# Half of a gMLP's u projection as seven Strassen block products, and one set of operand forms built two tiles earlier

## The chip, the cores and the metric

The kernel runs on one core of a Trainium2 chip. The metric is the device time of one launch in microseconds (us). Measurements of this kernel agree with each other to about 0.03%; 0.2% of its time, 3.9 us, is taken here as what can be told from no change.

The engines of the core: TensorE (PE in the profile, with PEld for its weight loads), VectorE (DVE), ScalarE (ACT), GpSimd (POOL) and SyncE (SP), which starts the transfers. Every engine works through its own list of instructions in order and waits on semaphores of the others.

## The reference

A decoder trunk with two layers over 544 columns: 512 of a prompt and 32 of a sample (8 sequences of 4). Only the part around the change matters here:

```python
h = h + 0.5 * swiglu(rmsnorm(h, ffn1_norm[i]), ffn1_w1[i], ffn1_w3[i], ffn1_w2[i])
xn = rmsnorm(h, mix_norm[i])                 # layer 0: the gMLP mixer
u, v = jnp.split(xn @ w_in, 2, axis=-1)      # w_in: 1024 x 2048
v = rmsnorm(v, v_norm)                       # v of the sample is an output too (gmlp_v_sample)
s = jnp.einsum('gts,bnsgd->bntgd', ws, vg)   # per chunk of 128 positions, lower triangle
h = h + (u * (s + b_s)) @ w_out
h = h + 0.5 * swiglu(rmsnorm(h, ffn2_norm[i]), ffn2_w1[i], ffn2_w3[i], ffn2_w2[i])
```

Layer 1 has attention in place of the mixer. All arithmetic is to be as exact as float32.

## The kernel before, in words

Everything is held transposed: a 1024-wide activation is 8 tiles of 128 features by 544 columns. A float32 product is made of three fp32r matmuls, high parts by high parts (line L285), high by low (L289) and low by high (L291), for each of 8 slices of 128 inputs and each of the two halves of 272 columns. A plain output tile of 128 features thus takes 48 matmuls of 272 columns, all added up in one PSUM buffer of the pool `ps`. This pool has three buffers of two banks; a second pool `pb` has two of one bank.

Weights come as tiles of 128 x 1024 by transfers that SP starts (L208), and are split ahead of their use: ACT rounds to the high part (L241), DVE subtracts to get the low part (L242). `self.ahead` holds how many such units ahead the split, the sums of blocks and the load stand.

The feed-forward parts (FFN) use Strassen's scheme (in Winograd's form) for their wide products: seven products of blocks, called "1", "5", "6", "2", "7", "3", "4" in the order of the work, give four output tiles of 128 x 544, each product being 24 matmuls (L538) instead of the 32 that they would share of eight. Three accumulators are used: A (a `ps` buffer; products 1, 6, 7, 4, one after the other into the same sums), C (a `ps` buffer; 5, then 3) and B (the two `pb` buffers; 2). After "1", "5" and "6" ACT copies the accumulator out (L546) before the next product may add to it. After "2", "7" and "3" DVE adds such a copy to the sums (L553, L555, L557), and after "4" ACT copies the result out (L560). The four block weights are plain pieces; the other three are sums of these, made on DVE (L227). The right-hand operand needs "forms", sums of the blocks of the activations: `forms()` makes them for two feature tiles at a time, by 2 ACT scalings (L351), 3 DVE sums (L355, L357, L358), 2 ACT casts and 2 DVE subtractions (L329, L330). There are four such sets per FFN. The first FFN of a layer-0 pass and its second are preceded by two plain pairs of tiles (`plain=2`: four plain tiles, copied by ACT at L471), and `more()` spreads the sets of forms over these tiles.

The gMLP (`gmlp`) works in this order:
- the eight v tiles, each taken out of PSUM by DVE with the norm's factor (L644), and squared by ACT for v's own norm (L368, summed by POOL at L370);
- the u tiles 0, 1, 2 (L656), then two transposes of v tiles (`v_turn`: each five small matmuls, L665 and L666, into a `ps` buffer, copied out by ACT at L668 and L669);
- the u tiles 3 to 7 with between them the other transposes and the spatial products (`spatial`: L676 and L679 on PE, L687, L690 and L694 on DVE);
- the eight output tiles (L714 adds them to the residual), which at once prepare the second FFN (`on_chunk`), its forms 1 to 3 among them.

DVE multiplies v by its norm's factor (L659), and takes the sample's 32 columns of each v tile (L661) into a small buffer of a pool of four, from where SP sends them out (`out_gv`).

Outside the FFN's product steps a list scheduler sets the order of each engine's instructions; within the product steps the order is as written.

Of the kernel before, what the change touches and what calls it, by code (L numbers as in the profile page):

```python
# [29 lines left out]
P = 128  # L30
# [62 lines left out]
def turns(out):  # L93

    return out.rearrange("p (b a) -> p b a", a=2)
# [42 lines left out]
class Builder:  # L138
# [207 lines left out]
    def forms(self, h, gcol, n, xs):  # L346

        nc = self.nc
        x = self.big()
        for a in range(2):  # L350
            nc.scalar.activation(x[:, a, :], h[2 * n + a], AF.Copy, scale=self.gain(gcol + 2 * n + a))  # L351
        t13, t24 = self.tmp(), self.tmp()
        two = lambda t: t.rearrange("p (a b) -> p a b", a=2)
        f13, f24 = self.big(F32R), self.big(F32R)
        nc.vector.tensor_tensor(two(t13), x[:, :, HT:], two(x[:, 0, :]), ALU.subtract)  # L355
        self.split_pair(f13, t13)
        nc.vector.tensor_tensor(t24[:, :HT], x[:, 1, HT:], t13[:, :HT], ALU.subtract)  # L357
        nc.vector.tensor_tensor(t24[:, HT:], x[:, 1, :HT], t24[:, :HT], ALU.subtract)  # L358
        self.split_pair(f24, t24)
        half = lambda t, b: tuple(x[:, b * HT:(b + 1) * HT] for x in t)  # L360
        f13, f24 = ((t[:, 0, :], t[:, 1, :]) for t in (f13, f24))
        return {"1": half(xs[2 * n], 0), "2": half(xs[2 * n + 1], 0), "3": half(xs[2 * n + 1], 1),
                "5": half(f13, 0), "7": half(f13, 1), "6": half(f24, 0), "4": half(f24, 1)}
    def ssq(self, acc, h, cols=slice(0, T), first=False):

        nc = self.nc
        sq = acc[:, cols] if first else self.tmp()[:, cols]
        nc.scalar.activation(sq, h[:, cols], AF.Square)  # L368
        if not first:
            nc.gpsimd.tensor_tensor(acc[:, cols], acc[:, cols], sq, ALU.add)  # L370
# [80 lines left out]
    def ffn(self, h, box, gcol, rstd, on_chunk, plain=1):  # L451

        nc, eng = self.nc, mybir.EngineType
        self.ahead = (2, 3, 6)
        first, xs, xf = [], self.pairs(box), box["f"]

        def more(n):
            if len(xf) < min(n, NKP):
                xf.append(self.forms(h, gcol, len(xf), xs))
        hid, todo = {}, ([], [])  # L460
        lead = plain == 1 and len(xf) < 3
        for f in range(2 * plain):
            g = self.big()
            for w in range(2):
                if lead:
                    more(len(xf) + 1)
                if rstd is None:
                    p, rstd = self.tile_rstd(xs, box["acc"])
                else:
                    p = self.tile_mm(xs)  # L470
                nc.scalar.copy(halves(g[:, w]), whole(p))  # L471
                for t in todo:
                    if t:
                        t.pop(0)()
                if not lead:
                    more((2 * f + w + 1) // plain)
            first.append((f // 2, f % 2, g))
            if f % 2 and f < 2 * plain - 1 or lead and f == 0:
                for j, a, g in first:
                    todo[a].extend(self.gate(hid, rstd, j, a, g))  # L480
                first = []
        assert self.chain is None
        for j, a, g in first:
            todo[a].extend(([None] * 3 if j == 0 else []) + self.gate(hid, rstd, j, a, g))
        with self.tc.manual_schedule(engines={eng.PE, eng.Activation, eng.DVE, eng.Pool}):
            self.ffn_steps(h, xf, rstd, hid, todo, plain, on_chunk)
        self.ahead = (2, 2, 4)
        self.pins = 2
        return rstd
# [127 lines left out]
    def gmlp(self, h, box, on_chunk):  # L617
# [13 lines left out]
        for g in range(NH):  # L631
            nc.gpsimd.tensor_tensor(wss[:NS, g * NS:(g + 1) * NS], wss[:NS, g * NS:(g + 1) * NS],
                                    self.c[:NS, C_TRI4:C_TRI4 + NS], ALU.mult)
        rstd, sq, v = None, self.st(), []
        for c in range(NC_):
            if rstd is None:
                p, rstd = self.tile_rstd(xs, box["acc"])
            else:
                p = self.tile_mm(xs)
            if c % 2 == 0:  # L640
                vt = self.big()

            def take(p=p, vc=vt[:, c % 2, :]):
                nc.vector.tensor_tensor(halves(vc), whole(p), halves(rstd), ALU.mult)  # L644
                self.ssq(sq, vc, first=not v)
                v.append(vc)
            self.evac(take)
        m, us = [None] * NC_, {}
        vts = {}

        def u_tile(c):
            p = self.tile_mm(xs)
            if c % 2 == 0:
                us["t"] = self.big()
            us[c] = us["t"][:, c % 2, :]
            nc.vector.tensor_tensor(halves(us[c]), whole(p), halves(rstd), ALU.mult)  # L656

        def v_turn(c):
            nc.vector.tensor_tensor(v[c], v[c], rv, ALU.mult)  # L659
            vs = self.sm(NS)  # L660
            nc.vector.tensor_scalar(vs, v[c][:, SEQ:], self.gain(G_GV + c), None, ALU.mult)  # L661
            nc.sync.dma_start(out=self.o["gv"][c], in_=vs)
            t = self.ps()
            for j in range(4):
                nc.tensor.transpose(t[:, 0, j * P:(j + 1) * P], v[c][:, j * P:(j + 1) * P], self.ident)  # L665
            nc.tensor.transpose(t[:NS, 1, :P], v[c][:, SEQ:], self.ident)  # L666
            vt = self.big()
            nc.scalar.copy(vt[:, 0, :SEQ], t[:, 0, :])  # L668
            nc.scalar.copy(vt[:NS, 1, :P], t[:NS, 1, :P])  # L669
            vts[c] = (vt[:, 0, :], vt[:, 1, :])  # L670
# [25 lines left out]
                self.split_pair(pair, sg)  # L696
                m[c] = pair[:, 0, :], pair[:, 1, :]

        u_tile(0)
        rv = self.rstd(sq)  # L700
        u_tile(1)
        u_tile(2)
        assert self.chain is None
        v_turn(0)
        v_turn(1)
        for c, spatials, turns in ((3, (0,), (2, 3)), (4, (1,), (4,)), (5, (2, 3), (5,)), (6, (4, 5), (6, 7)),
                                   (7, (6, 7), ())):
            u_tile(c)
            for k in turns:
                v_turn(k)  # L710
            spatial(*spatials)
        for c in range(NC_):
            p = self.tile_mm(m)
            nc.vector.tensor_tensor(halves(h[c]), whole(p), halves(h[c]), ALU.add)  # L714
# [655 lines left out]
    def build(self):  # L1370
# [3 lines left out]
        def plain(aps):  # L1374
            for ap in aps:
                self.add_plain(ap)

        def ple_units(n):
            for c in range(NC_):
                self.add_plain(i["wg"][n, c])  # L1380
                if c < 2:
                    self.add_plain(i["wp"][n, c])

        self.ffn_pieces(0)
        plain([i["win"][NC_ + c] for c in range(NC_)] + [i["win"][c] for c in range(NC_)])
        plain(i["wout"][c] for c in range(NC_))
        self.ffn_pieces(1)
        ple_units(0)
# [87 lines left out]
def _stationary(w):  # L1476

    k, m = w.shape
    return np.ascontiguousarray(
        w.reshape(k // P, P, m // P, P).transpose(2, 1, 0, 3).reshape(m // P, P, k // P * P))  # L1480
# [5 lines left out]
    return w.reshape(k // 256, 2, P, m // 256, 2, P).transpose(3, 4, 1, 2, 0, 5).reshape(m // 256, 4, P, k // 256, P)  # L1486


def _constants():
    c, d = np.zeros((P, NCONST), np.float32), np.zeros((P, NPASS), np.float32)  # L1490
    r = np.arange(P)
    c[:, C_ID:C_ID + P] = np.eye(P)
    d[:, C_NEG + P:C_NEG + 2 * P] = np.where(r[None, :] > r[:, None], NEG, 0.0)
    d[:, C_TRI:C_TRI + P] = r[:, None] <= r[None, :]
    d[:, C_TRI + P:C_STRICT] = 1
    d[:, C_STRICT:C_STRICT + P] = r[:, None] > r[None, :]
    d[:, C_PICK:C_PICK + NH] = r[:, None] % NS == NQ * np.arange(NH)[None, :]
    b4, hd, q = r // 32, r // 4 % 8, r % 4
    for k in range(4):
        c[:, C_ROLE + k] = q == k  # L1500
    c[:, C_ROLE + 4] = -(q == 0).astype(np.float32)
    c[:, C_ROLE + 5] = -(q == 1).astype(np.float32)
    c[:, C_ROLE + 6] = q >= 2
    c[:, C_ROLE + 7] = q < 2
    c[:, C_ROLE + 8] = hd == b4
    c[:, C_ROLE + 9] = hd == b4 + 4
    for k in range(4):
        c[:, C_B4 + k] = b4 == k
        c[:, C_SEL + k] = q == k
        c[:, C_NEGQ + k] = np.where(k > q, NEG, 0.0)  # L1510
    for k in range(8):
        c[:, C_H + k] = hd == k
    s = np.arange(NS)
    c[:, C_SUM:C_SUM + NS] = r[:, None] % NS == np.arange(NS)[None, :]
    c[:NS, C_TRI4:C_TRI4 + NS] = (s[:, None] // 4 == s[None, :] // 4) & (s[:, None] <= s[None, :])
    d[P - NS:, C_TRI4S:C_TRI4S + NS] = c[:NS, C_TRI4:C_TRI4 + NS]
    return c, d


def _arrays(x_prompt, x_sample, p_prompt, p_sample, cache_k, cache_v, cache_logf, page_table, ffn1_norm, ffn1_w1,  # L1520
# [9 lines left out]
    for w1, w3, w2, n in ((ffn1_w1, ffn1_w3, ffn1_w2, 0), (ffn2_w1, ffn2_w3, ffn2_w2, 0),  # L1530
# [9 lines left out]
    a["wp"] = np.stack([_stationary(w).reshape(2, 4, P, 2 * P).transpose(0, 2, 1, 3).reshape(2, P, 8 * P)  # L1540
                        for w in ple_w_proj])
    a["win"], a["wout"] = _stationary(gmlp_w_in[0]), _stationary(gmlp_w_out[0])
    a["wk"] = _stationary(w_kvf[:, :D])

    a["wv"] = w_kvf[:, D:2 * D].reshape(2, 4, P, 4, 256).transpose(3, 0, 2, 1, 4).reshape(8, P, 1024)
# [50 lines left out]
```

## Time and profile before

| | before |
|---|---|
| median of 3 runs | 1931.98 us (1931.47 to 1932.03) |
| the profiled execution | 1931.48 us, its span 1929.7 us |
| TensorE's granted clock over the span | 1.00 |
| PE busy, DVE busy, ACT busy in the span | 1906.5, 1457.5, 950.2 us |
| first FFN | to 356 us of the span |
| gMLP: v tiles; u tiles, transposes and spatial products; output tiles | 356 to 401; to 462; to 506 us |
| second FFN: plain tiles; product steps | from 506; from 529 us |

Times of instructions are counted from the span's start. A row of the timeline holds start, duration, engine, line, operation, output and input, and in brackets the idle time of this engine before it with what ended it. A row of the waits holds what waited for what, the sum, the count and the longest. A row of windows holds, for each of PE, PEld, DVE, ACT and POOL, the busy time and the number of instructions, then the granted clock, the share of the transfer engines and their rate.

### The profile page before, as it was taken

What the parts mean: (1) busy time and instruction counts of PE and PEld (TensorE: products, weight loads), DVE (VectorE), ACT (ScalarE), POOL (GpSimd) and SP (SyncE); (2) the same over time, 40 slices, a digit from 0 to 9 for tenths busy, and PEclk for the clock granted to TensorE, in tenths of its full rate; (3) what the DMA queues carried; (4) which work ended last, traced back from release to release, by engine and by line L of the source; (5) the groups of instructions that cost most, each with busy time, mean ns of one, the idle gap of its engine ahead of it and who ended that gap; (6) DMA issues with size and microseconds to landing.
All of it is one profiled execution on the core that took longest, in us unless ns stands there. A gap on an engine that the chain in (4) does not pass through costs nothing.

```text
span 1929.7 us, 39007 instructions
## 1 busy us (share of the span) xinstructions
PE 1906.5 (99%) x16508; PEld 1872.2 (97%) x16508; DVE 1457.5 (76%) x1799; ACT 950.2 (49%) x1396; POOL 142.6 (7%) x190
## 2 busy tenths in 40 slices
PE   9999999999999999999999999999999999999999
PEld 8999999999999999999999999999977899999999
DVE  7887877556788877766578887877476888878774
ACT  7544434424554444454466454444374754444461
POOL 0000000410100000023000000001131300000020
PEclk9999999999999999999999999999999999999999
DMA  5233234312223233431484232324769332332431
GB/s 195 79 112 121 84 123 147 108 48 88 88 88 107 86 120 105 153 104 45 144 306 157 103 129 69 129 86 136 217 210 341 101 110 81 112 113 86 139 109 47
DMA packets 98048, 237.62 MB, mean 123 GB/s; under 512 B 12130, under 2 KB 29826, under 8 KB 97874
## 3 DMA queue, kind: packets, MB, share of 16 engines
q1 hardware_dynamic: 97730, 235.09, 36.9%
q8 instruction: 130, 2.13, 0.5%
q14 instruction: 44, 0.36, 0.1%
q10 hardware_dynamic: 144, 0.04, 0.0%
HBM read 218.65 MB, written 16.44 MB: 122 GB/s over the span
## 4 chain that ended last, share of the span: by engine, by line
PE 89%; DVE 6%; ACT 3%; issue 1%; DMA 1%; POOL 0%; SPq 0%; ACTq 0%; DVEq 0%; POOLq 0%
PE ps L538 31%; PE ps L285 15%; PE ps L291 15%; PE ps L289 15%; PE pb L538 5%; DVE big L242 2%; ACT big L241 1%; DVE big L227 1%; DMA big<-in_cv 1%; PE ps L891 1%; PE ps L892 1%; PE ps L893 1%; DVE big L496 0%; DVE big L330 0%; PE ps L1285 0%
## 5 line engine op out<-in xcount | busy, mean ns | idle before, releaser
L538 PE MATMUL ps<-big,big 128*128 128x272 f32 x5616 | 668.8, 279 | 5.9 <-DVE big L555 3.5
L538 PEld LDWEIGHTS ps<-big,big 128*128 128x128 f32 x5616 | 658.5, 189 | 7.0 <-issue 4.0
L242 DVE TENSOR_TENSOR big<-big,big 128x1024 fp32r<-128x1024 f32 (+2 forms) x505 | 582.8, 1157 | 93.4 <-ACT big L241 92.9
L241 ACT CAST big<-big 128x1024 fp32r<-128x1024 f32 (+2 forms) x505 | 483.1, 977 | 326.5 <-DVE big L227 251.9
L285 PE MATMUL ps<-big,big 128*128 128x272 f32 x2668 | 531.3, 280 | 3.8 <-ACT big L241 2.3
L291 PE MATMUL ps<-big,big 128*128 128x272 f32 x2668 | 529.2, 280 | 1.8 <-DVE big L242 1.7
L289 PE MATMUL ps<-big,big 128*128 128x272 f32 x2668 | 528.3, 279 | 0.0
L285 PEld LDWEIGHTS ps<-big,big 128*128 128x128 f32 x2668 | 408.3, 189 | 8.5 <-ACT big L241 5.7
L291 PEld LDWEIGHTS ps<-big,big 128*128 128x128 f32 x2668 | 407.9, 189 | 3.6 <-DVE big L242 3.1
L289 PEld LDWEIGHTS ps<-big,big 128*128 128x128 f32 x2668 | 407.9, 189 | 0.0
L370 POOL TENSOR_TENSOR st<-st,tmp 128x544 f32<-128x544 f32 (+1 forms) x63 | 87.5, 1389 | 1476.7 <-ACT tmp L368 1476.5
L227 DVE TENSOR_TENSOR big<-big,big 128x1024 f32<-128x1024 f32 x156 | 190.2, 1219 | 0.0
L577 DVE SCALAR_TENSOR_TENSOR big<-ps,big 128x544 f32<-128x544 f32 x128 | 92.5, 723 | 104.0 <-PE ps L291 103.0
L546 ACT COPY tmp<-ps 128x544 f32<-128x544 f32 x117 | 71.6, 612 | 107.5 <-PE ps L538 107.2
L496 DVE TENSOR_TENSOR big<-big,st 128x1088 f32<-128x1088 f32 x88 | 113.2, 1289 | 3.3 <-ACT big L560 2.0
L538 PE MATMUL pb<-big,big 128*128 128x272 f32 x936 | 114.8, 279 | 0.0
L538 PEld LDWEIGHTS pb<-big,big 128*128 128x128 f32 x936 | 111.3, 189 | 0.0
L499 ACT ACTIVATE big<-big 128x544 f32<-128x544 f32 x88 | 58.0, 660 | 88.1 <-DVE big L496 88.0
L341 ACT ACTIVATE big<-big,gains 128x544 fp32r<-128x544 f32 (+1 forms) x80 | 55.3, 703 | 90.3 <-DVE big L577 55.0
L330 DVE TENSOR_TENSOR big<-big,big 128x544 fp32r<-128x544 f32 (+1 forms) x112 | 79.4, 715 | 22.8 <-ACT big L329 22.6
L342 DVE SCALAR_TENSOR_TENSOR big<-big,gains,big 128x544 fp32r<-128x544 f32 (+1 forms) x80 | 64.6, 817 | 23.4 <-ACT big L341 23.4
L329 ACT CAST big<-big 128x544 fp32r<-128x544 f32 (+1 forms) x112 | 71.2, 644 | 11.9 <-DVE big L502 7.5
(218 smaller groups left out, 1388.5 us busy)
## 6 DMA issues: line engine op xcount, KB each, us to landing
big<-in_w SPq DMA_DIRECT2D x156, 512.0 KB
big<-in_w2b SPq DMA_DIRECT2D x96, 384.0 KB
big<-in_w13p SPq DMA_DIRECT2D x16, 512.0 KB
big<-in_w2a SPq DMA_DIRECT2D x16, 512.0 KB
big<-in_win SPq DMA_DIRECT2D x16, 512.0 KB
big<-in_wg SPq DMA_DIRECT2D x16, 512.0 KB
big<-in_ck SPq DMA_DIRECT2D x16, 512.0 KB
big<-in_cv SPq DMA_DIRECT2D x16, 512.0 KB
```

The costliest lines, as they stand in the source:

```text
L227: self.nc.vector.tensor_tensor(t, a, b, ALU.add if op == "+" else ALU.subtract)
L241: self.nc.scalar.copy(hi, src)
L242: self.nc.vector.tensor_tensor(lo, src, hi.bitcast(F32), ALU.subtract)
L285: i = nc.tensor.matmul(o, wh, xh[:, b], start=s, stop=False)
L289: nc.tensor.matmul(o, wh, xl[:, b], start=False, stop=False)
L291: nc.tensor.matmul(o, wl, xh[:, b], start=False, stop=e)
L330: self.nc.vector.tensor_tensor(pair[:, 1, cols], src, pair[:, 0, cols].bitcast(F32), ALU.subtract)
L370: nc.gpsimd.tensor_tensor(acc[:, cols], acc[:, cols], sq, ALU.add)
L496: tt(g, g, rstd.unsqueeze(1).broadcast_to([P, 2, T]), ALU.mult)
L538: nc.tensor.matmul(turns(dst[w]), a[:, c], woven(b), start=k in "152" and kp == 0 and n == 0, stop=kp == NKP - 1 and n == 2, skip_group_ch ...
L546: nc.scalar.copy(t["r" + k], t["C" if k == "5" else "A"])
L577: nc.vector.scalar_tensor_tensor(halves(h[c]), whole(out), 0.5, halves(h[c]), ALU.mult, ALU.add)
```

## The change

First, the u tiles 0 to 3 are no longer four plain tiles. They become the seven block products of Strassen's scheme, in a new function `strassen`, with the same three accumulators, ACT copies and DVE sums as in the FFN. The weights come in another layout (`win7`), four tiles as before, and three sums of blocks are made on DVE. Four sets of forms are made of the mixer's input, one behind each of the first four v tiles. The plain u tile 4 stands first, so that v's norm can be worked out; then the products 1 and 5, then 6, 2, 7, 3, 4 with the transposes of v tiles 0; 1, 2; 3; 4, 5; 6 written behind them; then u tiles 5, 6, 7 with the last transpose and the spatial products.

Second, in an FFN with two plain pairs `more()` now asks for all four sets of forms at each tile where there are fewer than three. This moves the fourth set in both FFNs of layer 0.

```diff
+    def strassen(self, xf, done):
+        ...
+        def step(k):
+            hi, lo = self.unit()
+            self.advance()
+            if k == "2":
+                t["B"] = [self.pb()[:, :HT] for _ in range(2)]
+            elif k in "15":
+                t["A" if k == "1" else "C"] = self.ps()[:, :, :HT]
+            out = t["A" if k in "1674" else "C" if k in "53" else "B"]
+            for kp in range(NKP):
+                xh, xl = xf[kp][k]
+                for n, (a, b) in enumerate(((hi, xh), (hi, xl), (lo, xh))):
+                    for w in range(2):
+                        c = slice(512 * w + P * kp, 512 * w + P * kp + P)
+                        nc.tensor.matmul(turns(out[w] if k == "2" else out[:, w]), a[:, c], woven(b), ...)
+            if k in "156":
+                t["r" + k] = self.tmp().rearrange("p (w b) -> p w b", w=2)
+                nc.scalar.copy(t["r" + k], out)
+            elif k == "2":
+                t["g"] = self.big(), self.big()
+                for w in range(2):
+                    tt(halves(t["g"][0][:, w, :HT]), unwoven(out[w]), unwoven(t["r1"][:, w]), ALU.add)
+            elif k == "7":
+                tt(h4(t["g"][1][:, :, HT:]), u4(out), u4(t["r5"]), ALU.add)
+            elif k == "3":
+                tt(h4(t["g"][0][:, :, HT:]), u4(out), u4(t["r6"]), ALU.add)
+                done(0, t["g"][0])
+            else:
+                nc.scalar.copy(h4(t["g"][1][:, :, :HT]), u4(out))
+                done(1, t["g"][1])
+        return step
 ...
-                    more((2 * f + w + 1) // plain)
+                    more((2 * f + w + 1) // plain if len(xf) < 3 else NKP)
 ...
             self.evac(take)
+            if c < 4:
+                uf.append(self.forms(h, G_MIX, c, xs))
+            if c == 3:
+                self.ahead = (2, 3, 6)
 ...
-        u_tile(0)
+        def u_done(a, g):
+            nc.vector.tensor_tensor(g, g, rstd.unsqueeze(1).broadcast_to([P, 2, T]), ALU.mult)
+            for w in range(2):
+                us[2 * w + a] = g[:, w]
+
+        u_tile(4)
         rv = self.rstd(sq)
-        u_tile(1)
-        u_tile(2)
+        step = self.strassen(uf, u_done)
+        step("1")
+        step("5")
         assert self.chain is None
-        v_turn(0)
-        v_turn(1)
-        for c, spatials, turns in ((3, (0,), (2, 3)), (4, (1,), (4,)), (5, (2, 3), (5,)), (6, (4, 5), (6, 7)),
-                                   (7, (6, 7), ())):
+        for k, cs in zip("62734", ((0,), (1, 2), (3,), (4, 5), (6,))):
+            step(k)
+            for c in cs:
+                v_turn(c)
+        self.ahead = (2, 2, 4)
+        for c, groups in ((5, ((0, 1),)), (6, ((2, 3), (4,))), (7, ((5, 6), (7,)))):
             u_tile(c)
-            for k in turns:
-                v_turn(k)
-            spatial(*spatials)
+            if c == 5:
+                v_turn(7)
+            for cs in groups:
+                spatial(*cs)
 ...
-        plain([i["win"][NC_ + c] for c in range(NC_)] + [i["win"][c] for c in range(NC_)])
+        plain([i["win"][NC_ + c] for c in range(NC_)] + [i["win"][4]])
+        seven([i["win7"][x] for x in range(4)])
+        plain(i["win"][5 + c] for c in range(3))
```

The new lines that the text names: L383 is the products' matmul, L388 the ACT copies, L392, L394, L396 DVE's sums behind "2", "7", "3", L399 the ACT copy behind "4", L743 the multiplication by the norm's factor in `u_done`. The transposes are now at L708 and L709, their copies at L711 and L712, L702 is v times its factor, and L592, L594 are what L553, L555 were in the FFN.

How the scheduler places it is seen in three places. The first is PE between u tiles 2 and 3 of the kernel before: two transposes and a spatial product stand there (`ps_5041` and `ps_5054` are the transposes of v tiles 2 and 3, into different buffers), between two long plain tiles.

```order
L291 MATMUL ps_4987<-big_4253,big_4839 128x272 x2
L665 MATMUL ps_5041<-consts,big_4465 128x128 [waits PE_49,Activation_49]
L665 MATMUL ps_5041<-consts,big_4465 128x128 x3
L666 MATMUL ps_5041<-consts,big_4465 32x128
L665 MATMUL ps_5054<-consts,big_4465 128x128 [waits PE_49,Activation_49]
L665 MATMUL ps_5054<-consts,big_4465 128x128 x3
L666 MATMUL ps_5054<-consts,big_4465 32x128
L676 MATMUL ps_5063<-big_4260,big_4965 128x128 [waits DMAHW3_49,DVE_49,Pool_49]
```

After the change PE comes to four transposes in a row (of two of them the further rows are left out), of v tiles 2 to 5, behind product "3" (into `ps_4941`, accumulator C) and ahead of product "4" (into `ps_4906`, accumulator A, which holds the sums of "7").

```order
L383 MATMUL ps_4941<-big_4253,big_5016 128x272 x2
L708 MATMUL ps_5068<-consts,big_4493 128x128 [waits PE_49,Activation_49]
L708 MATMUL ps_5068<-consts,big_4493 128x128 x3
L709 MATMUL ps_5068<-consts,big_4493 32x128
L708 MATMUL ps_5112<-consts,big_4493 128x128 [waits DVE_49]
L709 MATMUL ps_5112<-consts,big_4493 32x128
L708 MATMUL ps_5157<-consts,big_4646 128x128 [waits PE_49,Activation_49]
L709 MATMUL ps_5157<-consts,big_4646 32x128
L708 MATMUL ps_5170<-consts,big_4646 128x128 [waits PE_49,Activation_49]
L709 MATMUL ps_5170<-consts,big_4646 32x128
L383 MATMUL ps_4906<-big_4355,big_5077 128x272 [waits DVE_49]
```

The transposes have moved together, at a place where A and C hold two of the three `ps` buffers. On ACT their copies stand around a cast of a weight (`big_5077`, the high part for "4"):

```order
L711 COPY big_5074<-ps_5068 128x512 [waits PE_49]
L712 COPY big_5074<-ps_5068 32x128
L241 CAST big_5077<-big_4595 128x1024 [waits DMAHW3_49]
L711 COPY big_5118<-ps_5112 128x512 [waits PE_49]
L712 COPY big_5118<-ps_5112 32x128
```

So the copy of v tile 3 (`ps_5112`) comes behind that cast. On DVE, the sum behind "3" (L396) stands ahead of the sum behind "7" (L394), with u's factor and the low part for "4" between them:

```order
L396 TENSOR_TENSOR big_5047<-ps_4941,tmp_5000 128x2x272 [waits PE_49]
L743 TENSOR_TENSOR big_5047<-big_5047,st_4338 128x1088 [waits DVE_49]
L242 TENSOR_TENSOR big_5078<-big_4595,big_5077 128x1024 [waits Activation_49]
L394 TENSOR_TENSOR big_5048<-ps_4906,tmp_4966 128x2x272
```

L394 is what "4" waits for, and it now stands fourth in this row.

The second place is DVE at the start of the second FFN. Before, the fourth set of forms stood between two sums of blocks, behind the copy of the third plain tile:

```order
L227 TENSOR_TENSOR big_6178<-big_6122,big_5987 128x1024
L355 TENSOR_TENSOR tmp_6233<-big_6230 128x544
L357 TENSOR_TENSOR tmp_6234<-big_6230,tmp_6233 128x272
L358 TENSOR_TENSOR tmp_6234<-big_6230,tmp_6234 128x272
L330 TENSOR_TENSOR big_6235<-tmp_6233,big_6235 128x544
L330 TENSOR_TENSOR big_6236<-tmp_6234,big_6236 128x544
L242 TENSOR_TENSOR big_6272<-big_6178,big_6271 128x1024
```

After the change it stands behind the first plain tile, among the few instructions of the norm's factor (L442, L427, L430, L431):

```order
L442 TENSOR_TENSOR tmp_6094<-st_5563,tmp_6093 128x544
L355 TENSOR_TENSOR tmp_6117<-big_6114 128x544
L357 TENSOR_TENSOR tmp_6118<-big_6114,tmp_6117 128x272
L427 SCALAR_TENSOR_TENSOR tmp_6104<-st_6103 128x544
L358 TENSOR_TENSOR tmp_6118<-big_6114,tmp_6118 128x272
L330 TENSOR_TENSOR big_6119<-tmp_6117,big_6119 128x544
```

It has moved past the low parts of two weights and two sums; the sum that was ahead of it is now followed at once by the low part that needs it.

The third place is DVE late in the plain tiles of the first FFN. Before:

```order
L227 TENSOR_TENSOR big_657<-big_597,big_333 128x1024
L330 TENSOR_TENSOR big_709<-big_175,big_709 128x544
L330 TENSOR_TENSOR big_712<-big_328,big_712 128x544
L355 TENSOR_TENSOR tmp_718<-big_715 128x544
L357 TENSOR_TENSOR tmp_719<-big_715,tmp_718 128x272
L496 TENSOR_TENSOR big_592<-big_592,st_243 128x1088
L358 TENSOR_TENSOR tmp_719<-big_715,tmp_719 128x272
```

After:

```order
L227 TENSOR_TENSOR big_597<-big_393,big_395 128x1024
L355 TENSOR_TENSOR tmp_656<-big_653 128x544
L357 TENSOR_TENSOR tmp_657<-big_653,tmp_656 128x272
L358 TENSOR_TENSOR tmp_657<-big_653,tmp_657 128x272
L330 TENSOR_TENSOR big_658<-tmp_656,big_658 128x544
L330 TENSOR_TENSOR big_659<-tmp_657,big_659 128x544
L242 TENSOR_TENSOR big_668<-big_597,big_667 128x1024
```

There the set moved one sum of blocks up, and with it out of the queue behind the gate (L496).

More of the change, by code (lines that the diff above doesn't have):

```diff
@@ L363, in forms @@
                 "5": half(f13, 0), "7": half(f13, 1), "6": half(f24, 0), "4": half(f24, 1)}
+    def strassen(self, xf, done):
+        nc, tt, t = self.nc, self.nc.vector.tensor_tensor, {}
+        u4 = lambda t: t.rearrange("p w (b a) -> p w a b", a=2)
+        h4 = lambda t: t.rearrange("p w (a b) -> p w a b", a=2)
+        def step(k):
[11 more added lines that the diff above has]
+                        c = slice(512 * w + P * kp, 512 * w + P * kp + P)
+                        nc.tensor.matmul(turns(out[w] if k == "2" else out[:, w]), a[:, c], woven(b),
+                                         start=k in "152" and kp == 0 and n == 0, stop=kp == NKP - 1 and n == 2,
+                                         skip_group_check=True)
+            if k in "156":
[14 more added lines that the diff above has]
+        return step
     def ssq(self, acc, h, cols=slice(0, T), first=False):
@@ L633, in gmlp @@
                                     self.c[:NS, C_TRI4:C_TRI4 + NS], ALU.mult)
-        rstd, sq, v = None, self.st(), []
+        rstd, sq, v, uf = None, self.st(), [], []
         for c in range(NC_):
@@ L1376, in plain, with seven @@
                 self.add_plain(ap)
+        def seven(aps):
+            d = self.seven(aps)
+            self.pieces.extend(d[k] for k in SEVEN)
         def ple_units(n):
@@ L1486, in _blocks, with _pairs @@
     return w.reshape(k // 256, 2, P, m // 256, 2, P).transpose(3, 4, 1, 2, 0, 5).reshape(m // 256, 4, P, k // 256, P)
+def _pairs(w):
+    h = w.shape[1] // 2
+    return np.stack([_blocks(w[:, :h]), _blocks(w[:, h:])], 3).reshape(4, P, 1024)
 def _constants():
@@ L1542, in _arrays @@
     a["win"], a["wout"] = _stationary(gmlp_w_in[0]), _stationary(gmlp_w_out[0])
+    a["win7"] = _pairs(gmlp_w_in[0][:, :D // 2])
     a["wk"] = _stationary(w_kvf[:, :D])
```

## The prediction

> **What bounds the kernel now.** I read the page's busy shares first, then the chain of work that ended last, then windows by stage.
>
> ```profile
> span 1929.7 us, 39007 instructions
> PE 1906.5 (99%) x16508; PEld 1872.2 (97%) x16508; DVE 1457.5 (76%) x1799; ACT 950.2 (49%) x1396; POOL 142.6 (7%) x190
> PE 89%; DVE 6%; ACT 3%; issue 1%; DMA 1%; POOL 0%; SPq 0%; ACTq 0%; DVEq 0%; POOLq 0%
> 200.00:400.00 200.00, 200.00 (x1729) 200.00 (x1729) 141.99 (x156) 89.96 (x119) 26.95 (x29) 1.00 0.33 109
> 356.50:401.20 44.70, 44.70 (x388) 44.70 (x387) 20.98 (x22) 16.21 (x21) 17.32 (x23) 1.00 0.21 67
> 401.20:462.00 60.80, 60.80 (x513) 59.48 (x513) 38.45 (x62) 18.29 (x33) 1.34 (x1) 1.00 0.26 81
> 506.00:528.80 22.80, 22.80 (x199) 22.80 (x198) 13.25 (x17) 10.36 (x15) 1.35 (x1) 1.00 0.16 50
> 528.80:575.00 46.20, 43.32 (x372) 42.98 (x371) 40.87 (x48) 25.99 (x35) 0.00 (x0) 1.00 0.32 102
> ```
>
> PE is busy 99% of the span at clock 1.00 and carries 89% of the chain. In the gMLP's v tiles (356.5 to 401.2) and in the u tiles with transposes and spatial products (401.2 to 462) it isn't idle at all. So a matmul taken out there is worth its whole pitch, and nothing else is to be had; any wait put in there is a loss in full. Where PE does wait is in the FFNs' product steps:
>
> ```profile
> PE ps L538 <- DVE big L555: 2.1, 1, 2.1
> PEld ps L538 <- issue: 2.3, 1, 2.3
> PEld ps L285 <- ACT big L241: 0.9, 1, 0.9
> PEld ps L285 <- ACT big L241: 1.1, 2, 0.8
> PEld ps L538 <- ACT tmp L546: 0.8, 1, 0.8
> ```
>
> The first three rows are the waits in 500 to 575 us (second FFN), the last two those in 22 to 80 us (first FFN). By the weight loads, PE stands 2.3 us in the second FFN, between products "3" and "4", for DVE's sum behind "7" (L555), and once more 0.9 us for a cast. In the first FFN it stands 0.8 us for the ACT copy behind "1" (L546), and 0.8 us at most for a late cast.
>
> **Matmuls taken out.** Four plain u tiles are 4 x 48 = 192 matmuls, seven products 7 x 24 = 168; all are of 272 columns. The bound stretch 200 to 400 us holds 1729 matmuls in 200.00 us, 0.1157 us each. 24 fewer: -2.78 us. Transposes, spatial products and the rest of PE's list stay in number.
>
> **What DVE and ACT get in exchange.** Prices, from the page's groups and from the timeline of the fourth set of forms in the second FFN:
>
> ```profile
> L242 DVE TENSOR_TENSOR big<-big,big 128x1024 fp32r<-128x1024 f32 (+2 forms) x505 | 582.8, 1157 | 93.4 <-ACT big L241 92.9
> L227 DVE TENSOR_TENSOR big<-big,big 128x1024 f32<-128x1024 f32 x156 | 190.2, 1219 | 0.0
> L496 DVE TENSOR_TENSOR big<-big,st 128x1088 f32<-128x1088 f32 x88 | 113.2, 1289 | 3.3 <-ACT big L560 2.0
> 527.37 0.72 DVE L355 TENSOR_TENSOR tmp<-big 128x544 f32<-128x544 f32 x1
> 528.12 0.44 DVE L357 TENSOR_TENSOR tmp<-big,tmp 128x272 f32<-128x272 f32 x1
> 528.60 0.44 DVE L358 TENSOR_TENSOR tmp<-big,tmp 128x272 f32<-128x272 f32 x1
> 528.95 0.72 DVE L330 TENSOR_TENSOR big<-tmp,big 128x544 fp32r<-128x544 f32 x1
> 530.19 0.73 DVE L330 TENSOR_TENSOR big<-tmp,big 128x544 fp32r<-128x544 f32 x1 [0.52 <-ACT big L329]
> 395.78 0.72 DVE L644 TENSOR_TENSOR big<-ps,st 128x544 f32<-128x544 f32 x1 [4.83 <-PE ps L291]
> 401.34 0.72 DVE L644 TENSOR_TENSOR big<-ps,st 128x544 f32<-128x544 f32 x1 [1.41 <-PE ps L291]
> ```
>
> A set of forms is 0.72 + 0.44 + 0.44 + 0.72 + 0.73 = 3.05 us of DVE, four sets 12.2. The products add three sums of blocks (3 x 1.22), three more low parts (3 x 1.16), the sums behind "2", "7", "3" and two factors (2 x 1.29), and drop four evictions: about 10 net (my estimate). In the v tiles DVE waits 4.83 and 1.41 us in turn for PE, 6.2 in two tiles of 5.57 us, where two sets need 6.1. PE does not wait for v's evictions at once, since a second `ps` buffer is being filled meanwhile: I take 0 here. If the cover is gone, a late eviction costs its excess; from zero to 1 us over the four tiles. In 401.2 to 462 DVE is busy 38.5 of 60.8 us and has room for 10 more, but not at every point; that is the next term. On SP the load of one later weight (for u tile 7) moves between the first two `out_gv` issues. What it waits for is long past, so nothing queues behind it. DVE's third to eighth sample columns (now L704) wait for such transfers; before, that cost DVE 1.8 us at most. By adding up DVE's list from product "1" on, I have the last of them done some 0.5 us ahead of L396, so 0, and up to 1 us if not.
>
> **The four transposes in a row.** This is where I expect a loss. Rows of the kernel before for a transpose and its copies:
>
> ```profile
> 418.28 0.60 PE L665 MATMUL ps<-consts,big 128*128 128x128 f32 x4
> 418.82 0.60 PE L665 MATMUL ps<-consts,big 128*128 128x128 f32 x4
> 419.02 0.59 ACT L668 COPY big<-ps 128x512 f32<-128x512 f32 x1 [9.99 <-PE ps L666]
> 419.51 0.25 ACT L669 COPY big<-ps 32x128 f32<-32x128 f32 x1
> 420.30 1.04 ACT L241 CAST big<-big 128x1024 fp32r<-128x1024 f32 x1
> L555 DVE TENSOR_TENSOR big<-ps,tmp 128x544 f32<-128x544 f32 x39 | 28.2, 723 | 26.5 <-PE ps L538 26.5
> ```
>
> A transpose is 0.54 us of PE (418.28 to 418.82); its copy begins 0.74 after it began and ends 0.74 later (419.02 to 419.76). Let S be the end of "3". A and C hold two buffers, so:
> - v2 has a free buffer: S to S+0.54; its copies end at about S+1.5.
> - v3 needs C, freed by L396: starts on DVE at S+0.2, 0.72 long, so S+1.0; PE waits 0.46. It ends at S+1.54.
> - v4 needs v2's buffer, free at S+1.5: no real wait; ends at S+2.1.
> - v5 needs v3's buffer. On ACT v3's copies stand behind the cast of "4" (1.04), which begins after v2's copies, at S+1.45: 2.5, then 0.74: S+3.2. PE waits about 1.1; v5 ends at S+3.75.
> - "4" needs L394. On DVE: L396 to S+0.85, the factor (pitch 1.2) to 2.05, the low part, which waits for the cast, 2.55 to 3.75, L394 to S+4.45 or so. PE waits 0.75 or a little less.
>
> With 0.1 to 0.2 for the low part of "3", these make 2.4 us. The bounds: 0, if the one wait in the steps is hidden as all are in 401.2 to 462 now; and 8.2, if each of four transposes waits for the whole round of 0.54 + 0.74 + 0.04 for signals with a cast of 1.04 ahead of each copy, less its own 0.54 in the sum already, that is some 1.8 to 2.1 each. I take +2.4, as both engines' lists are known and only their pace is not.
>
> **The fourth set of forms, second FFN.**
>
> ```profile
> 525.09 1.23 DVE L242 TENSOR_TENSOR big<-big,big 128x1024 fp32r<-128x1024 f32 x1 [5.92 <-ACT big L241]
> 535.75 1.23 DVE L242 TENSOR_TENSOR big<-big,big 128x1024 fp32r<-128x1024 f32 x1 [1.11 <-ACT big L241]
> 539.28 1.23 DVE L242 TENSOR_TENSOR big<-big,big 128x1024 fp32r<-128x1024 f32 x1 [1.17 <-ACT big L241]
> 546.92 0.72 DVE L555 TENSOR_TENSOR big<-ps,tmp 128x544 f32<-128x544 f32 x1
> 523.50 0.61 ACT L471 COPY big<-ps 128x544 f32<-128x544 f32 x1 [5.00 <-PE ps L291]
> 524.01 1.05 ACT L241 CAST big<-big 128x1024 fp32r<-128x1024 f32 x1
> ```
>
> The set lies in DVE's chain (527.37 to 530.92, 3.5 us with its gap); moved behind the first plain tile it falls into the 5.92 us that DVE is idle up to 525.09. That idle time does not shrink otherwise: the cast at 524.01 stands on ACT behind the copy of a plain tile (523.50). From 525.09 on, the chain of sum, cast and low part runs on. It gets less than 3.5 back, because casts stand on ACT behind the copies of "1" and "5", which wait for PE's steps. Walking both lists, the low part now at 539.28 comes at 536.9, 2.4 earlier, and L555 with it, at 544.5 to 544.9. "3" ends on PE at 545.37; with 0.63 for L555 and a signal, PE stands some 0.26 us where it stood 2.31. So -2.05 us. Ends: -1.2 if casts hold the chain by one step more (1.05 of the gain lost), -3.2 if the next wait of 0.9 goes too. I leave that one: DVE is without a gap from 540 to 565, and PE comes 2 us earlier as well.
>
> **The same set, first FFN.**
>
> ```profile
> 60.22 0.65 ACT L329 CAST big<-tmp 128x544 fp32r<-128x544 f32 x1 [1.44 <-DVE tmp L358]
> 60.77 1.99 ACT L241 CAST big<-big 128x1024 fp32r<-128x1024 f32 x2
> 62.66 0.60 ACT L546 COPY tmp<-ps 128x544 f32<-128x544 f32 x1
> ```
>
> The forms' second cast waited 1.44 us for DVE; behind it came two casts of weights, and behind these, 62.66, the copy that "6" waits for. With the forms earlier by one sum and out of the gate's way, these move up by 1.4, the copy ends near 61.9, ahead of the end of "5" at 62.4. -0.8 us; ends 0 and -1.6 (the other wait of 0.8, for a cast behind a sum, which I leave).
>
> **Sum.** -2.78 + 2.4 - 2.05 - 0.8 = -3.23. The profiled execution took 1931.48, so 1928.25; it lies 0.50 below the median, so I forecast 1928.8 for the median. The bound for "no change", 3.86 us, lies close by, at 1928.1 (and 1935.8).
>
> **Rivals.**
> 1. The transposes hide better and another FFN wait goes as well: -2.78 + 1 - 3.2 - 0.8 = -5.8, 1926.2. For it: no PE wait at all in 401 to 462 now. Against: three buffers with two held.
> 2. Full serialization on the one buffer, price 8.2: -2.78 + 8.2 - 2.05 - 0.8 = +2.6, 1934.6; slower by over 0.2% from a price of 9.5 on, for instance when the sample columns' transfers hold L396 by a further 1.8. Against: v2 and v4 need no cast.
> 3. The forms' move does not do what it is for: ACT holds the casts at the tiles' copies (row 523.50) and the FFNs gain nothing: -2.78 + 2.4 = -0.4, 1931.6. For: the chain must gain 2 us through three casts that ACT orders. Against: DVE is without gap from 540 on.
> 4. The clock falls. The 2.3 us stop at 545 left it at 1.00 in the row of 528.8 to 575. If the stops among the transposes halved it for the next product, 24 x 0.1157 = 2.8 more: -0.4, 1931.6. The Trainium skill says something of the kind in "TensorE: Matmul & The Clock Gate", section "A second HAM failure mode: psum-queue depth-cycling": short idle times of PE between groups that cycle through PSUM make the clock swing between half and full. This trace does not agree so far, by that row.
>
> **Chances.** Forecast 0.61, its own range 1926.6 to 1930.8; rival 1: 0.14; rival 2: 0.09; rival 3: 0.14; rival 4: 0.02. Faster by over 0.2%: all of rival 1 and four tenths of the forecast, 0.38. Slower: most of rival 2 lies within 0.2%, so 0.05 from its upper part and 0.02 for what I don't see. Range: from 1925.4, between rival 1 and the sum of all best ends (-2.78 + 0 - 3.2 - 1.6 = -7.6, 1924.4), to 1932.8, beyond rival 3 and short of rival 2.
>
> **What would show it.** 24 fewer matmuls; PE waits of 0.3 to 1.3 us for L396, for the copies L711 and L712 and for L394, all before "4"; none in the v tiles; in the second FFN a wait of under 0.7 for L594; none for the copy behind "1" in the first FFN; the 0.9 still there. It is wrong if waits of the transposes come to over 4 us, or if PE still stands over 1 us for L594.

## The result, and the profile after

The changed kernel took 1927.99 us (median of 18, 1927.02 to 1929.18), the kernel before 1931.38 us in the same comparisons (18, 1930.51 to 1932.54): 3.39 us less, ratio 0.9983 with a 95% interval of 0.9977 to 0.9989. The forecast was 1928.8 us, 3.2 us less. The difference came out to within 0.2 us; the time itself is 0.8 us lower than forecast, mostly because the median of three runs that I counted from lay 0.6 above that of 18. The 18 runs of a kernel spread over 2 us, 0.1%, not 0.03%. The gain, 0.18%, is under the 0.2% that I took as the bound for no change, but its interval is clear of zero. Two terms of the sum did not have the size I gave them, and that they nearly cancel is luck.

From the page of the kernel after: span, busy shares, and the chain of work that ended last.

```profile
span 1926.9 us, 39017 instructions
PE 1901.6 (99%) x16484; PEld 1866.5 (97%) x16484; DVE 1481.5 (77%) x1828; ACT 965.2 (50%) x1419; POOL 145.9 (8%) x190
PE 89%; DVE 6%; ACT 2%; DMA 1%; issue 1%; SPq 0%; POOL 0%; DVEq 0%; ACTq 0%; POOLq 0%
```

24 matmuls fewer (16508 to 16484), 24 us more of DVE, 15 more of ACT; PE still carries the chain. The profiled execution took 1928.75 us, 0.76 above its median. Windows of the kernel after: v tiles with forms, products with transposes, product steps of the second FFN.

```profile
356.50:399.50 43.00, 43.00 (x374) 43.00 (x373) 35.40 (x42) 25.37 (x36) 18.98 (x23) 1.00 0.19 65
404.90:432.10 27.20, 24.58 (x208) 23.50 (x207) 23.61 (x36) 13.96 (x26) 0.00 (x0) 1.00 0.30 102
527.40:575.00 47.60, 46.87 (x404) 46.63 (x403) 42.58 (x48) 25.55 (x35) 0.00 (x0) 1.00 0.27 89
```

In the v tiles DVE went from 21 busy us of 45 to 35 of 43, and PE does not wait at all: the cover held. Among the products PE is idle 2.6 of 27.2 us, where it was never idle before. In the second FFN it is idle 0.7 of 47.6, against 2.9 of 46.2 before. The waits of the weight loads, first in 350 to 470 us, then (last row) in 500 to 575 us:

```profile
PEld ps L708 <- DVE big L396: 1.5, 1, 1.5
PEld ps L383 <- DVE big L394: 1.0, 1, 1.0
PEld ps L708 <- ACT big L712: 0.6, 1, 0.6
PEld ps L383 <- DVE big L242: 0.6, 1, 0.6
PEld ps L285 <- ACT big L241: 0.9, 1, 0.9
```

The four waits are those forecast: L396, L394, a transpose's copy and the low part for "3". Measured between the starts of neighbouring matmuls, less the usual pitch, they are 1.42, 0.91, 0.45 and 0.52: 3.3 us, where I had 2.4. (The table below agrees: 0.41 us more in the gMLP, with 2.78 us of matmuls gone, is 3.2 lost.) The wait before product "4" of the second FFN (2.3) is gone, and the 0.9 behind it has stayed.

One column for each stage makes the rest readable. The columns hold differences between the starts of the small matmuls that add up a norm's factor, read from the timelines (such matmuls stand in the first tiles of the first FFN, the gMLP, the second FFN and the part behind it):

| kernel | first factor at | first FFN | gMLP | second FFN | from there to the span's end |
|---|---|---|---|---|---|
| before | 25.99 | 336.69 | 149.91 | 343.55 | 1073.6 |
| before_again_1 | 24.59 | 337.34 | 149.90 | 344.25 | 1073.5 |
| before_again_2 | 24.21 | 337.10 | 149.90 | 344.25 | 1074.1 |
| after | 24.65 | 336.23 | 150.32 | 341.30 | 1074.4 |
| strassen_only | 24.99 | 336.77 | 150.13 | 344.25 | 1074.2 |
| forms_only | 24.54 | 336.17 | 149.90 | 341.30 | 1073.9 |
| forms_second_ffn_only | 24.22 | 337.04 | 149.90 | 341.29 | 1074.2 |
| eight_small_buffers | 24.69 | 336.03 | 148.43 | 341.30 | 1073.0 |
| turns_spread | 24.60 | 335.91 | 147.26 | 341.29 | 1073.7 |
| spread_and_eight | 24.09 | 336.40 | 147.69 | 341.29 | 1072.8 |

The gMLP, the larger part of the change, lost 0.4 us; the second FFN gained 2.25 against the profile that I had, the first FFN about 0.8 (mean of the five with the old order 336.99, of the five with the new 336.15). No part of the change touches the first and the last column, and the kernel before itself shows 24.2 to 26.0 in the first and 1073.5 to 1074.1 in the last: I take their differences as chance. Whether the two lowest of the last column (1073.0 and 1072.8, both kernels with eight small buffers) are chance too, no run shows.

### The profile page after: what moved, and what is told of

Read it like the earlier page. It is cut to its first block, busy times and chain, and to the rows that moved or that the text cites. A ratio compares the mean times of both kernels' runs of the same rounds, so it can differ in the third digit from the quotient of the medians.

```text
span 1926.9 us, 39017 instructions
## 1 busy us (share of the span) xinstructions
PE 1901.6 (99%) x16484; PEld 1866.5 (97%) x16484; DVE 1481.5 (77%) x1828; ACT 965.2 (50%) x1419; POOL 145.9 (8%) x190
## 4 chain that ended last, share of the span: by engine, by line
PE 89%; DVE 6%; ACT 2%; DMA 1%; issue 1%; SPq 0%; POOL 0%; DVEq 0%; ACTq 0%; POOLq 0%
PE ps L577 32%; PE ps L285 15%; PE ps L291 15%; PE ps L289 15%; PE pb L577 5%; DVE big L242 2%; DVE big L227 1%; PE ps L943 1%; ACT big L241 1%; PE ps L944 1%; PE ps L945 1%; PE ps L1337 0%; DMA big<-in_cv 0%; DVE big L330 0%; PE ps L719 0%
## 5 line engine op out<-in xcount | busy, mean ns | idle before, releaser
L577 PE MATMUL ps<-big,big 128*128 128x272 f32 x5616 | 668.5, 279 | 3.1 <-ACT tmp L585 1.7
L577 PEld LDWEIGHTS ps<-big,big 128*128 128x128 f32 x5616 | 658.4, 189 | 3.9 <-ACT tmp L585 2.1
L285 PE MATMUL ps<-big,big 128*128 128x272 f32 x2604 | 517.1, 280 | 3.7 <-ACT big L241 2.1
L291 PE MATMUL ps<-big,big 128*128 128x272 f32 x2604 | 515.6, 279 | 2.5 <-DVE big L242 2.4
L289 PE MATMUL ps<-big,big 128*128 128x272 f32 x2604 | 514.4, 279 | 0.5 <-DVE big L342 0.5
L285 PEld LDWEIGHTS ps<-big,big 128*128 128x128 f32 x2604 | 397.4, 189 | 8.1 <-ACT big L241 4.5
L291 PEld LDWEIGHTS ps<-big,big 128*128 128x128 f32 x2604 | 397.1, 189 | 4.5 <-DVE big L242 3.9
L289 PEld LDWEIGHTS ps<-big,big 128*128 128x128 f32 x2604 | 396.8, 189 | 0.9 <-DVE big L342 0.9
L227 DVE TENSOR_TENSOR big<-big,big 128x1024 f32<-128x1024 f32 x160 | 196.2, 1226 | 0.0
```

What stands on the lines that cost most here:

```text
L227: self.nc.vector.tensor_tensor(t, a, b, ALU.add if op == "+" else ALU.subtract)
L285: i = nc.tensor.matmul(o, wh, xh[:, b], start=s, stop=False)
L289: nc.tensor.matmul(o, wh, xl[:, b], start=False, stop=False)
L291: nc.tensor.matmul(o, wl, xh[:, b], start=False, stop=e)
L577: nc.tensor.matmul(turns(dst[w]), a[:, c], woven(b), start=k in "152" and kp == 0 and n == 0, stop=kp == NKP - 1 and n == 2, skip_group_ch ...
```

## The experiments

**The parts apart.** In `strassen_only` the line in `more()` is as before; in `forms_only` only this line is changed:

```diff
-                    more((2 * f + w + 1) // plain)
+                    more((2 * f + w + 1) // plain if len(xf) < 3 else NKP)
```

> The change's first part alone (block products in the gMLP), with the forms where they were before. My theory: the gMLP by itself gains nothing, since the 2.78 us of matmuls taken out are given back as PE waits around the row of transposes (3.3 us in the trace of the changed kernel); so +0.4 us against before, 1931.4 to 1932.4, ratio about 1.0002. Rival: the gain of the whole comes from the matmuls, the waits lying in time that PE lost somewhere anyway; then -2 to -3 us, ratio 0.9985 to 0.999. The waits of 2.3 us (sum behind 7) and 0.8 us (copy behind 1) of the FFNs should stand in the trace as before.

> The change's second part alone: the kernel before with the fourth set of forms moved. My theory: this carries the whole gain, -2.3 (second FFN, the wait before product 4 gone) and -0.8 to -0.95 (first FFN, the wait before product 6 gone): about -3.1 us, ratio 0.9984. Rival (the third of the prediction): the FFNs gain nothing of note, 0 to -0.5 us.

Measured (before: 1931.26, 24 runs): `strassen_only` 1931.74, ratio 1.0000 (0.9991 to 1.0010); `forms_only` 1927.45, ratio 0.9981 (0.9972 to 0.9990). The block products by themselves gain nothing that can be told, as my theory had it, and the rival (the matmuls carry the gain) is out. The forms' move carries the whole gain, and by its median more than the 3.1 us I expected, 3.8. In `strassen_only` the FFNs' waits stand as before (weight loads, 500 to 575 us and 22 to 80 us):

```profile
PEld ps L577 <- issue: 2.3, 1, 2.3
PEld ps L577 <- ACT tmp L585: 0.9, 1, 0.9
```

**The forms of the second FFN alone.** The condition is `if len(xf) < 3 or plain == 2`, so that the first FFN stays as it was.

> The kernel before with the set of forms moved in the second FFN alone. By the trace of the changed kernel the wait before product 4 (2.31 us) goes, and the first FFN keeps its wait of 0.8 us before product 6: -2.3 us, ratio 0.9988. With runs in which the stop is followed by a slow clock, the mean gain is larger, up to -2.9 us. Rival: the first FFN's part carries more than its 0.8 us, and this one is under 2 us.

Measured: 1927.77 against 1931.09, ratio 0.9981 (0.9972 to 0.9990), 3.3 us less. The second FFN carries nearly all, and more than the 2.31 us of the wait. The first FFN's part is 0.3 by the medians of the two kernels, which their intervals can't tell from its 0.8 in the stage table.

**Why more than the wait: the clock, in part.** The kernel before, twice more, for a second and third profile.

> The kernel before, for a second profile. Question: how much of its profiled start, where PE reached its first norm factor at 25.99 us against 24.5 to 25.0 us in five other profiles whose start has the same instructions, is chance, and whether the stop of 2.3 us before product 4 in the second FFN, after which the clock stayed at 1.00 in the first profile but fell to 0.50 for some 4 us in the one with the block products alone, is followed by a slow stretch here. Theory one (chance of the alignment): the start at 24.5 to 25.5 us, and either answer on the clock; stop of 2.2 to 2.4 us. Theory two (something in the changed kernels): 26 us again and clock 1.00 again.

> The same kernel a third time, for the same question; with both, three profiles of the stop and of the start. If theory one holds, the three starts differ by about 1 us and at least one of the stops may be followed by a clock of 0.50.

The two took 1931.34 and 1931.42 us. Their starts were 24.59 and 24.21: the 25.99 of the first profile was chance, so theory one holds (24.21 lies a little under its 24.5). And the clock did fall. Windows of before_again_1, then the same windows of the first profile of before; the third number from the end is the granted clock:

```profile
544.00:547.00 3.00, 0.89 (x8) 0.69 (x7) 3.00 (x4) 0.72 (x1) 0.00 (x0) 1.00 0.00 0
547.00:549.00 2.00, 1.97 (x10) 2.00 (x11) 2.00 (x3) 1.58 (x3) 0.00 (x0) 0.57 0.00 0
549.00:551.00 2.00, 2.00 (x12) 2.00 (x12) 2.00 (x4) 0.49 (x1) 0.00 (x0) 0.58 0.00 0
551.00:553.00 2.00, 2.00 (x20) 2.00 (x19) 2.00 (x4) 1.80 (x3) 0.00 (x0) 1.00 0.18 18
```

```profile
547.00:549.00 2.00, 1.21 (x10) 1.24 (x11) 2.00 (x5) 1.66 (x3) 0.00 (x0) 1.00 0.00 0
549.00:551.00 2.00, 2.00 (x20) 2.00 (x19) 2.00 (x2) 0.65 (x2) 0.00 (x0) 1.00 0.00 0
```

After the same stop of 2.3 us, PE did 12 matmuls in 549 to 551 us here and 20 there. The stop was followed by such a stretch in three of its four profiles (both of these and `strassen_only`, 0.50 in the same window), and only the first, the one I had, escaped. None of the six profiles without the stop has such a stretch in 545 to 555. Finer windows show a stretch of 3.41 us at 0.50 in all three. It does not begin with PE's new start (at 547.03, 546.41 and 547.09) but 0.24, 1.34 and 0.96 us later, at 547.27, 547.75 and 548.05. In before_again_2 PE is at work at full clock first:

```profile
545.00:547.00 2.00, 0.59 (x5) 0.62 (x6) 2.00 (x4) 1.04 (x1) 0.00 (x0) 1.00 0.00 0
547.00:549.00 2.00, 2.00 (x14) 2.00 (x14) 2.00 (x3) 1.26 (x2) 0.00 (x0) 0.69 0.00 0
```

Why three fell and one did not is not shown by an experiment, but the traces fit one reading. In each of them the changes of the granted clock lie whole multiples of 3.413 us apart, as if the clock were decided once for each such stretch. In the three that fell, the stretch just ahead of the fall holds 2.30, 2.07 and 2.30 us of the stop. In the first profile, counted back in whole stretches from the clock's fall behind the last matmul (at 1928.55 us), a border lies at 546.15, inside the stop (545.48 to 547.79): no stretch holds more than 1.64 us of it.

The 96 matmuls behind the stop took 12.86 us (547.03 to 559.89) instead of 11.19: 1.67 lost, of which nearly 1.0 came back, because DVE then had time to get ahead and the next wait (0.9 by the weight loads) did not occur. Net 0.70, as the table's 344.25 and 343.55 say. So the forms' move is worth 2.25 or 2.95 us by the case.

How often each case comes is better read from all timed runs, since each has its mean granted clock, and 3.41 us at one half take 0.0009 from it. Of the 40 runs of the kernel before beside the experiments 19 have 1.000, 13 have 0.999 and 8 have 0.998, with medians of 1930.75, 1931.50 and 1931.81 us. Of the 59 runs of the six kernels without the stop 45 have 1.000, 14 have 0.999 and none less (`forms_only` has such a stretch in the first 12 us of its profile). That makes 0.72 slow stretches in a run with the stop and 0.24 without, so the stop is followed by one in about half of the runs, and costs 0.3 us on average by this (my estimate). With 2.25 for the wait that is 2.6, and with 0.84 for the first FFN 3.4, where 3.3 and 3.8 were measured. The rest is within the intervals (0.9972 to 0.9990 is 1.9 to 5.4 us less), so the clock is shown to be part of the excess, and not to be all of it.

**The row of transposes: what makes it.** In `eight_small_buffers` the sample's columns of v tiles 4 to 7 get buffers of their own:

```diff
-            vs = self.sm(NS)
+            vs = self.sm(NS) if c < 4 else self.sm(2 * NS)[:, :NS]
```

> The changed kernel, with eight small buffers for the sample's 32 columns of v instead of four (tiles 4 to 7 take theirs from a pool that is used later). Nothing on DVE then waits for an out_gv transfer, and the scheduler places the transposes otherwise: v2 within product 3, v3 and v4 behind it, v5 within product 4; the sum behind 7 comes ahead of that behind 3. My theory (the row of four comes of these buffers, and DVE's 2 us of waiting for the transfers delayed L396 by about 1 us): waits among the products 1.8 us or less instead of 3.3, so -1.0 to -2.3 us against the changed kernel, ratio to before about 0.9975. Rival (the waits come of two of three PSUM buffers being held, whatever stands on DVE): 3 us of waits as in the changed kernel, only at other places, ratio 0.9983.

Measured: 1925.54, ratio to before 0.9971 (0.9961 to 0.9982), 2.4 us under the changed kernel's median, of which the gMLP has 1.9 (148.43 instead of 150.32). DVE no longer waits for transfers, and two waits of PE are left (weight loads, 350 to 470 us; first row), and L394 now stands ahead of L396 (DVE's timeline, below):

```profile
PEld ps L708 <- ACT big L712: 1.7, 2, 1.1
```

```profile
424.90 0.72 DVE L394 TENSOR_TENSOR big<-ps,tmp 128x544 f32<-128x544 f32 x1
425.53 0.71 DVE L396 TENSOR_TENSOR big<-ps,tmp 128x544 f32<-128x544 f32 x1
```

The rival (3 us at other places, whatever stands on DVE) is out. That the wait for the transfers costs by itself, and that the order it leads to costs, are not told apart: the scheduler reorders when the buffers are there.

**The transposes spread.** In `turns_spread` they are written one product later, and the last three between the u tiles:

```diff
-        for k, cs in zip("62734", ((0,), (1, 2), (3,), (4, 5), (6,))):
+        for k, cs in zip("62734", ((), (0,), (1,), (2,), (3, 4))):
 ...
-            if c == 5:
-                v_turn(7)
+            for t in {5: (5, 6), 6: (7,)}.get(c, ()):
+                v_turn(t)
```

> The changed kernel with the transposes written one product later (v0 behind 2, v1 behind 7, v2 behind 3, v3 and v4 behind 4, v5 and v6 behind u tile 5, v7 behind u tile 6); four small buffers as before. At most two transposes now stand together while products hold A and C. My theory: waits of PE in the products fall to 0.5 us or less, -2.8 us against the changed kernel, ratio to before about 0.997. Rival: the work of DVE that is 10 us larger shows elsewhere (waits of the spatial products or of u tiles 6 and 7), and the gain is under 1 us.

Measured: 1924.02, ratio to before 0.9962 (0.9948 to 0.9975), 4.0 us under the changed kernel's median (expected: 2.8) and the lowest median of all kernels run. gMLP 147.26, 2.65 less than before: of the 2.78 us of matmuls all but 0.13 is now a gain. Against the changed kernel the gMLP gives 3.1 of the 4.0; the other 0.9 stands in columns of the table that this edit does not touch, and is not explained. The window of u tiles, products and spatial work shows PE without idle time, and the one wait left is a weight load's:

```profile
399.50:462.00 62.50, 62.50 (x526) 61.04 (x526) 50.21 (x79) 25.72 (x43) 1.34 (x1) 1.00 0.35 104
```

```profile
PEld ps L383 <- DVE big L394: 0.2, 1, 0.2
```

The rival (DVE's extra work shows elsewhere) is out: DVE is 50.2 of 62.5 us busy there and holds up nothing but the 0.2.

**Both together.**

> The transposes spread as in turns_spread, and eight small buffers as well. My theory (both remove the same waits, and with the transposes spread there are under 0.3 us left): no further gain, 0 to -0.3 us against turns_spread, 1923.7 to 1924.3, ratio to before 0.9962. Rival (they remove different waits): their gains of 2.4 and 4.0 us add up in part, -1 us or more against turns_spread, 1923 or less.

Measured: 1924.76, ratio 0.9966 (0.9954 to 0.9978): no gain over `turns_spread`, rather 0.7 more, of which 0.43 is seen in the gMLP. The runs of the two kernels overlap, so the 0.7 is not clear of noise. They remove the same waits, and by the trace the free buffers even cost 0.4 at one place. DVE ahead of L394, first in `turns_spread`, then with eight buffers, and PE's product "4" there:

```profile
421.38 0.23 DVE L704 TENSOR_SCALAR sm<-big,gains 128x32 f32<-128x32 f32 x1
422.66 0.72 DVE L394 TENSOR_TENSOR big<-ps,tmp 128x544 f32<-128x544 f32 x1
```

```profile
421.35 0.67 DVE L704 TENSOR_SCALAR sm<-big,gains 128x32 f32<-128x32 f32 x4
423.07 0.72 DVE L394 TENSOR_TENSOR big<-ps,tmp 128x544 f32<-128x544 f32 x1
423.84 3.05 PE L383 MATMUL ps<-big,big 128*128 128x272 f32 x24 [0.39 <-DVE big L394]
```

With nothing to wait for, three more of the small copies (0.44 us) went ahead of L394, and product "4" waited for it by 0.4.

## Why the prediction was right, point by point

**Matmuls (-2.78).** Right: 24 fewer, and `turns_spread` gets 2.65 of it.

**Forms in the v tiles (0).** Right, PE 43.00 of 43.00. DVE's extra work was listed one sum of blocks short: there are four more of them (156 before), not three. With four the prices in the text make 10.3 us, and 22.5 with the forms; 24.0 were measured.

```profile
L227 DVE TENSOR_TENSOR big<-big,big 128x1024 f32<-128x1024 f32 x160 | 196.2, 1226 | 0.0
```

**The row of transposes (+2.4).** Right in kind, 0.9 short. DVE, PE and ACT of the kernel after:

```profile
414.39 5.17 DVE L702 TENSOR_TENSOR big<-big,st 128x544 f32<-128x544 f32 x8
420.06 1.22 DVE L242 TENSOR_TENSOR big<-big,big 128x1024 fp32r<-128x1024 f32 x1
421.90 0.23 DVE L704 TENSOR_SCALAR sm<-big,gains 128x32 f32<-128x32 f32 x1
424.18 0.85 DVE L704 TENSOR_SCALAR sm<-big,gains 128x32 f32<-128x32 f32 x3 [2.05 <-DMA out_gv<-sm]
424.94 0.72 DVE L396 TENSOR_TENSOR big<-ps,tmp 128x544 f32<-128x544 f32 x1
428.04 0.72 DVE L394 TENSOR_TENSOR big<-ps,tmp 128x544 f32<-128x544 f32 x1
421.33 2.58 PE L383 MATMUL ps<-big,big 128*128 128x272 f32 x20 [0.35 <-DVE big L242]
423.75 0.60 PE L708 MATMUL ps<-consts,big 128*128 128x128 f32 x4
425.71 0.66 PE L708 MATMUL ps<-consts,big 128*128 128x128 f32 x4 [1.25 <-DVE big L396]
427.30 0.66 PE L708 MATMUL ps<-consts,big 128*128 128x128 f32 x4 [0.28 <-ACT big L712]
428.81 3.05 PE L383 MATMUL ps<-big,big 128*128 128x272 f32 x24 [0.74 <-DVE big L394]
425.14 1.04 ACT L241 CAST big<-big 128x1024 fp32r<-128x1024 f32 x1
426.52 0.59 ACT L711 COPY big<-ps 128x512 f32<-128x512 f32 x1 [0.34 <-PE ps L709]
```

The end of "3", S, is 423.75. L396 began at S+1.19 where I had S+0.2: DVE stood 2.05 us for an `out_gv` transfer. I had walked DVE's list and put the last small copy half a microsecond ahead of L396, with "up to 1 us if not"; it was the "if not". So v3's transpose waited 1.42 instead of 0.46. That delay then took away the next wait: the cast of "4" (425.14) was over before v3's copy (426.52) was due, so v5 waited 0.45, for v3's own copy, instead of 1.1. "4" came at S+5.06 (I had S+4.45). The low part for "3" cost 0.52 instead of 0.1 to 0.2, since DVE did all eight multiplications of v (L702, 5.17 us) ahead of it (420.06), where the prediction gave no walk of the list.

**The forms in the second FFN (-2.05).** The chain was right to a tenth: the low part came at 535.52 and L594 at 543.28. With the 1.39 us by which this part started earlier these are 536.9 and 544.7 on the clock of before (forecast: 536.9, and 544.5 to 544.9). L594 was then just in time, so no rest of 0.26 was left. (Part of the 0.26 was a slip: by the starts of the matmuls "3" ended at 545.48, not 545.37.)

```profile
512.46 0.73 DVE L355 TENSOR_TENSOR tmp<-big 128x544 f32<-128x544 f32 x1 [2.18 <-ACT big L351]
535.52 1.23 DVE L242 TENSOR_TENSOR big<-big,big 128x1024 fp32r<-128x1024 f32 x1 [1.17 <-ACT big L241]
543.28 0.72 DVE L594 TENSOR_TENSOR big<-ps,tmp 128x544 f32<-128x544 f32 x1
```

The term's size was off beyond that for a reason that the profile of before could not show: 2.25 by that profile, 2.95 by the other profiles of before, through the clock.

**The first FFN (-0.8).** Right in the traces (0.84). The copy behind "1" came 4.24 us after the first block product began (56.16), against 5.71 before, 1.5 earlier (forecast: 1.4), and the wait for it is gone.

```profile
60.40 0.60 ACT L585 COPY tmp<-ps 128x544 f32<-128x544 f32 x1
```

**The rivals.** The third (ACT holds the casts, the FFNs gain nothing) is refuted by `forms_only`. Of the first, the better hidden transposes came true only in `turns_spread`, with their order mended; the other half, one more FFN wait gone, came true nowhere (the 0.9 of the second FFN stands wherever the 2.3 is gone). The second did not come true at all: v2 and v4 had no wait. The fourth was put at the wrong place. Among the transposes, four stops of 0.5 to 1.4 us within 9 us left the clock at 1.00 (row 404.90); the rule that I cited from the Trainium skill ("TensorE: Matmul & The Clock Gate", "A second HAM failure mode: psum-queue depth-cycling") isn't borne out by stops of that size and number. But I used "the 2.3 us stop left it at 1.00" as evidence, and that was one execution's luck. The Trainium skill, "TensorE: Matmul & The Clock Gate", "Part 1: The HAM clock gate", names at least one idle window of about 3.4 us for the clock to fall. Here a stop of 2.3 us did it in three profiles of four, so the measurement decides.

**A correction to the description of the kernel.** `plain=2` holds for the first FFN alone (eight plain tiles); the second has `plain=1` and four. In the code the fourth set moves from behind the eighth tile to behind the seventh, and from behind the fourth to behind the first. And the new condition works the other way round than described: with fewer than three sets `more()` asks as before, and as soon as there are three it asks for all four at once. The quoted orders and the terms stand as they are.

## What to carry to other kernels

Matmuls saved at a place where the array never waited are a gain only if nothing new waits there: 2.78 us saved came with 3.3 us of new waits until the eight transposes were placed elsewhere. When a scheduler piles operations up, look for a small pool (here four buffers of 32 columns) that sets their order, and for short instructions that stand, waiting for a transfer, ahead of the one that frees an accumulator. When PE stands for 2 us, take more than one profile, since the stop may cost its length or its length and a slow stretch.

## What the runs showed of the hardware that was not expected

A stop of PE of 2.3 us was followed by 3.41 us at a granted clock of 0.50 in three profiles of the same stop out of four, and the fall came 0.24 to 1.34 us after PE had begun again, not during the stop. Four shorter stops (0.52, 1.42, 0.45, 0.91 us) within 9 us left the clock at 1.00. The start of the kernel varies by 1.9 us between executions (first norm factor at 24.09 to 25.99 us).
